# New instruction lengths and distances in the list scheduler of a decoder trunk's odd layer

## The chip, the cores and the metric

The kernel runs on one core of a Trainium2 chip. The metric is the device time of one execution in microseconds; the median of three runs of the kernel before is 2234.52 us (2234.44 to 2235.84). The core has five engines that work through their own queues in order: TensorE (PE, with its weight loads PEld), VectorE (DVE), ScalarE (ACT), GpSimd (POOL) and SyncE (SP), which here issues the DMAs. An engine waits for another by semaphores.

## What is computed

A trunk of two residual layers on x of 1024 tokens by 1024 features, float32, then a last RMS norm. The even layer (dilated attention and a gated linear recurrence) is not touched. The odd layer, cut to what matters:

```python
qkv, z, b_logit, a_logit = split(hn @ w_in)            # 4096, 2048, 16, 16 columns
qkv = silu(causal_depthwise_conv(qkv, conv_w))         # 4 taps
q, k, v = split(qkv)                                   # 8 heads of q and k, 16 of v, 128 wide
q, k = l2_normalize(q) * 128 ** -0.5, l2_normalize(k)
beta, g = sigmoid(b_logit), -exp(a_log) * softplus(a_logit + dt_bias)
# chunked delta rule: S_t = exp(g_t)(I - b_t k_t k_t^T) S_{t-1} + b_t k_t v_t^T ; o_t = S_t^T q_t
sol = triangular_solve(lower + eye, rhs)               # per chunk
v_new = u_n - w_n @ state; o = qd_n @ state + a_n @ v_new
state = state * gl_n + kt_n^T @ v_new
o = rms_norm(o, norm_w) * silu(z)
h = h + o @ w_out
out = rms_norm(h, final_norm_w)
```

## The kernel before, in words

The odd layer works on eight pairs of heads hh = 0 to 7 (one k and q head with its two v heads) and on eight chunks of 128 tokens each. Weights come as 128 x 512 pieces through `cut` (line 323): SP loads `raww`, ACT rounds it into `w_hi`, DVE subtracts into `w_lo`. Every projection is three fp32r matmul passes of 512 columns (hi x hi, hi x lo, lo x hi), 24 matmuls for half the tokens, in one of two PSUM banks with the tag `pj`. For each head there are these generators, which write their instructions in small steps:

- `proj(j)` (line 1182): first `way_out(j - 2)`, then the projections of k of head j + 1 (`pk`), of the two v heads (`pv`) and of q (`pq`). Each goes through `conv` (line 1103): ACT copies both halves into the single buffer `ub` (uk, uv, uq in the trace), scales one tap, DVE adds three taps with three dependent steps, ACT takes the tanh, and a last DVE step gates (kT, vT, q). `turn_q`, `turn_k` and `turn_v` transpose on PE (tq, tk, tv) and scale (`bv`, `sc`, `kn`); `turn_k` has a chain of small DVE steps (rn, rt).
- `invert(hh)` (line 1255): the triangular inverse. Sixteen DVE steps make L from kk, ACT gathers Lg, DVE transposes it into Lp, and a loop of 31 (line 1292) takes two dependent DVE steps each: tm from Lp and Tp, then Tp less tm. tm has one buffer. Two DVE transposes (Tn, Un) follow, and small matmuls (qp, up, q, u in the trace) put the blocks together in U, kept in the tile L.
- `recur(hh)` (line 1360): for each chunk, PE makes ks and qs from the state S, DVE makes r from ks, ACT makes oq from qs, PE makes vp from r and U, DVE makes vt and ACT makes vn from vp, PE makes kv from vt, and DVE makes the next S from kv. Beside this PE makes op from vn and qk for the next chunk, DVE adds bv and makes A, ACT squares bv into oj.
- `way_out(hh)` (line 1228): norm of bv on DVE (ors, ort) and POOL, the projection of z (`oz`), its gate g (one buffer), transposes ot, and on ACT, POOL and SP the product oy, which goes to `ymix` in DRAM. `out_last` (line 1466) reads `ymix` back (rawy, yplo), multiplies with the output weights (op from w_hi and w_lo) and adds into the residual hr.

`mix` (line 366) and `blend` (line 376) interleave these in program order: `recur(hh)` with `invert(hh + 1)` and `proj(hh + 1)`; ahead of the loop stand the gates, the projections of head 0 and `invert(0)`.

That program order is only the start. In the odd layer every call to an engine goes to `Plan.add`, and `plan.run()` (line 1492) makes a list schedule of all five queues. `edges` finds what each operation must wait for; for each reuse of a buffer it adds a gate, which opens when all users of the old tile are done. `times` (line 107) gives each operation two numbers: how long its engine is held, and when its result is there. `run` takes, again and again, the engine that can start first, and on it the ready operation that stands first in program order. `release` (line 227) says from when a follower may start: the end of what it waits for and a distance `SEM` (line 90) by the follower's engine. Line 270 then issues all operations in the order of their modelled starts. On the chip each queue runs in that order, whatever the true times are. Line 284 records the same calls in the even layer, which has no plan.

Of the kernel before, what the change touches and what calls it, by code (L numbers as in the profile page):

```python
# [16 lines left out]
PSUM = bass.MemoryType.PSUM  # L17
# [64 lines left out]
class Plan:  # L82
# [4 lines left out]

    SEM = {"PE": 500, "DVE": 300, "ACT": 300, "POOL": 300, "SP": 300}  # L90

    def __init__(self):
        self.ops = None
# [12 lines left out]

    def times(self, op, last):

        key, name, a = op["key"], op["name"], op["a"]
        n = self.elems(op["out"][0])  # L110
        if key == "SP":
            return 420, 3200
        if key == "PE":
            if name == "transpose":
                return 109, 280
            r32 = a[1].dtype == F32R
            rows, cols = a[2].ap[0][1], self.elems(a[1])
            small = rows < 128 or cols < 128
            if small:
                held = 2.0 * (8 if cols == 32 else 18)  # L120
            else:
                held = n / 2.4 * (1 if r32 else 4) + (14 if r32 else 8)
            if small != last.get("small", False):
                held += 120
            last["small"] = small
            return held, held + 190
        if key == "DVE":
            if name == "transpose":
                t = 1950 if n >= 1024 else 1070 if op["out"][0].ap[-1][0] != 1 or a[1].ap[-1][0] != 1 else 620
            elif name == "memset":  # L130
                t = 60 + 0.82 * n
            elif n < 20:
                t = 85
            elif n >= 512:
                t = 100 + 1.15 * n
            else:
                t = 70 + 1.08 * n
            return t, t + 80
        if key == "ACT":
            t = 210 + 0.75 * n if n > 128 else 300  # L140
            if "accum_out" in op["kw"]:
                t = 440
            return t, t + 95
        if name == "memset":
            return 560, 600
        t = 780 if n <= 256 or a[0].ap[0][1] == 32 else 1330
        return t, t + 40

    def edges(self):
        ops = self.ops  # L150
# [52 lines left out]
    def run(self):  # L203
        ops = self.ops
        pred, gates = self.dag = self.edges()
        n = len(ops)
        succ = [[] for _ in range(n + len(gates))]
        deg = [0] * (n + len(gates))
        for i, ps in enumerate(pred):
            for j in ps:  # L210
                succ[j].append(i)
                deg[i] += 1
        for g, (old, new, _) in enumerate(gates):
            inner = set(new)
            for j in old:
                succ[j].append(n + g)
                deg[n + g] += 1
            for i in new:
                if not pred[i] & inner:
                    succ[n + g].append(i)  # L220
                    deg[i] += 1
        keys = ("PE", "DVE", "ACT", "POOL", "SP")
        ready = {k: [] for k in keys}
        free = {k: 0.0 for k in keys}
        at = [0.0] * (n + len(gates))

        def release(j, done, key):
            for i in succ[j]:
                k = ops[i]["key"] if i < n else None
                if k is None or k == key and k not in ("PE", "SP"):  # L230
                    t = done
                else:
                    t = 0.0 if k == key == "PE" else done + self.SEM[k]
                at[i] = max(at[i], t)
                deg[i] -= 1
                if not deg[i]:
                    if i < n:
                        ready[k].append(i)
                    else:
                        release(i, at[i], None)  # L240

        for i in range(n):
            if not deg[i]:
                ready[ops[i]["key"]].append(i)
        last, starts, done_n, ends = {}, [0.0] * n, 0, [0.0] * n
        while done_n < n:
            best = None
            for k in keys:
                if ready[k]:
                    s = max(free[k], min(at[i] for i in ready[k]))  # L250
                    if best is None or s < best[0]:
                        best = s, k
            if best is None:
                raise RuntimeError("the order of the tiles' places does not work out")
            s, k = best
            i = min(i for i in ready[k] if at[i] <= s)
            ready[k].remove(i)
            held, got = self.times(ops[i], last)
            starts[i] = s
            free[k] = s + held  # L260
            ends[i] = s + got
            release(i, s + got, k)
            done_n += 1
        self.starts, self.ends = starts, ends
# [1298 lines left out]
```

## Time and profile before

| what | value |
|---|---|
| median of 3 runs | 2234.52 us |
| the profiled execution | 2235.39 us |
| its span, first to last instruction | 2233.6 us |
| mean granted clock of TensorE | 0.979 |
| PE, PEld busy | 2162.9 us (97%), 1780.9 us (80%) |
| DVE, ACT, POOL busy | 1393.5 us (62%), 947.2 us (42%), 239.2 us (11%) |

The profile is of one execution. Its times count from the span's start; the page cuts the span into 40 slices of 56 us and gives the busy tenths of each engine in them. The granted clock is the share of full speed at which PE was allowed to run. The first projections of the odd layer run at about 1240 us. A row of the timeline has start, length, engine, line, operation, output and inputs, shapes and count; in brackets stands how long the engine was idle before it and what ended that. The operations of the odd layer have line 270, so they are told apart by their tiles.

### The profile page before, as it was taken

To read this page: it belongs to the slowest core of one execution; us is meant where nothing else is said; L and a number is where in the kernel's file an instruction comes from. 1 tells how busy PE (TensorE), PEld (TensorE's weight loads), DVE (VectorE), ACT (ScalarE), POOL (GpSimd) and SP (SyncE) were. 2 spreads that over 40 slices of the span, in tenths; PEclk is the share of its full clock that TensorE was granted. 3 is DMA by queue.
4 is the path that set the end of the run, shared out by engine and by line. 5 is a ranking of instruction groups with operands and counts; after the bars stand their busy time and mean duration, and the time that the engine had idled before them with its cause. 6 is when DMAs were issued, how large, how long until landed. Compare 5 with 4: busy or idle time off the path is not lost. (4 is left out here: it accounts for less than half of the span.)

```text
span 2233.6 us, 52459 instructions
## 1 busy us (share of the span) xinstructions
PE 2162.9 (97%) x21781; PEld 1780.9 (80%) x21781; DVE 1393.5 (62%) x3236; ACT 947.2 (42%) x2551; POOL 239.2 (11%) x252
## 2 busy tenths in 40 slices
PE   7999999999999999989998998899999999999998
PEld 6888888888787878767786776788888888887886
DVE  6353545453444444446666798697897988865677
ACT  6233333333223222222124855657566565653223
POOL 0011111110000000000000001312212121130100
PEclk9999999999999999989998998799999999999999
DMA  4111111114333434362233212212213121224223
GB/s 149 39 49 45 48 44 49 49 39 122 84 102 93 114 104 115 92 171 88 92 100 108 87 46 55 70 48 79 79 57 83 49 83 53 83 74 150 89 95 123
DMA packets 100078, 184.14 MB, mean 82 GB/s; under 512 B 12672, under 2 KB 30208, under 8 KB 99840
## 3 DMA queue, kind: packets, MB, share of 16 engines
q1 hardware_dynamic: 99840, 180.79, 26.5%
q8 instruction: 171, 2.80, 0.5%
q14 instruction: 67, 0.55, 0.1%
HBM read 151.25 MB, written 29.49 MB: 81 GB/s over the span
## 5 line engine op out<-in xcount | busy, mean ns | idle before, releaser
L284 DVE TENSOR_TENSOR w_lo<-raww,w_hi 128x512 fp32r<-128x512 f32 x160 | 117.9, 740 | 150.0 <-ACT w_hi L284 149.5
L284 ACT CAST w_hi<-raww 128x512 fp32r<-128x512 f32 x160 | 99.4, 621 | 203.7 <-DMA raww<-in_ewo_dram 54.2
L270 PE MATMUL op<-w_hi,yplo 128*128 128x512 f32 x448 | 140.4, 392 | 0.7 <-DVE hr L270 0.6
L284 ACT ACTIVATE P<-P,nm 128x256 f32<-128x256 f32 (+7 forms) x128 | 71.4, 559 | 133.4 <-DVE nm L284 133.3
L270 ACT CAST w_hi<-raww 128x512 fp32r<-128x512 f32 x132 | 81.8, 621 | 89.8 <-DMA raww<-in_owo_dram 42.8
L270 DVE TENSOR_TENSOR hr<-hr,op 128x512 f32<-128x512 f32 x128 | 87.4, 685 | 48.7 <-PE op L270 46.2
L284 PE MATMUL op<-w_hi,yphi 128*128 128x512 f32 x320 | 105.9, 405 | 7.9 <-DVE hres L284 4.8
L270 DVE TENSOR_TENSOR w_lo<-raww,w_hi 128x512 fp32r<-128x512 f32 x132 | 96.3, 732 | 20.5 <-ACT w_hi L270 17.5
L270 PE MATMUL pv<-hn_hi,w_hi 128*128 128x512 f32 x256 | 107.4, 419 | 0.0
L270 PE MATMUL oz<-hn_hi,w_hi 128*128 128x512 f32 x256 | 107.3, 419 | 0.0
L270 PE MATMUL pv<-hn_hi,w_lo 128*128 128x512 f32 x256 | 103.6, 405 | 0.0
L270 PE MATMUL pv<-hn_lo,w_hi 128*128 128x512 f32 x256 | 102.4, 400 | 0.0
L270 PE MATMUL oz<-hn_hi,w_lo 128*128 128x512 f32 x256 | 102.2, 399 | 0.0
L270 PE MATMUL oz<-hn_lo,w_hi 128*128 128x512 f32 x256 | 101.9, 398 | 0.0
L284 DVE STREAM_TRANSPOSE PB<-P 128x256 f32<-128x256 f32 (+3 forms) x64 | 54.6, 853 | 72.9 <-ACT P L284 72.9
L270 PEld LDWEIGHTS op<-w_hi,yplo 128*128 128x128 f32 x448 | 84.1, 188 | 18.9 <-DVE hr L270 1.5
L270 POOL TENSOR_TENSOR gca<-gca,MA 128x256 f32<-128x256 f32 x64 | 54.6, 854 | 366.0 <-DMA gca<-gcd 196.3
L270 PE MATMUL op<-w_lo,yplo 128*128 128x512 f32 x224 | 86.9, 389 | 0.0
L284 DVE TENSOR_TENSOR hres<-hres,op 128x512 f32<-128x512 f32 x96 | 64.7, 682 | 31.7 <-PE op L284 30.9
L284 DVE CUSTOM_DVE_ANT_0 P<-S,G 128x256 f32<-128x256 f32 (+7 forms) x128 | 58.1, 491 | 36.8 <-PE S L284 36.5
L284 PEld LDWEIGHTS op<-w_hi,yphi 128*128 128x128 f32 x320 | 62.0, 194 | 23.8 <-DVE hres L284 5.6
L284 PE MATMUL avp<-w_hi,hn_hi 128*128 128x256 f32 x256 | 74.6, 291 | 0.0
(345 smaller groups left out, 6352.6 us busy)
## 6 DMA issues: line engine op xcount, KB each, us to landing
raww<-in_ew_dram SPq DMA_DIRECT2D x128, 256.0 KB, 3.0
raww<-in_ow_dram SPq DMA_DIRECT2D x100, 256.0 KB, 3.0
V<-vd SPq DMA_DIRECT2D x64, 256.0 KB, 5.3
rawy<-ymix SPq DMA_DIRECT2D x64, 256.0 KB, 2.7
raww<-in_ewo_dram SPq DMA_DIRECT2D x32, 256.0 KB, 3.0
gcl<-gcd SPq DMA_DIRECT2D x64, 128.0 KB, 3.2
gca<-gcd SPq DMA_DIRECT2D x64, 128.0 KB, 3.0
ymix<-oy SPq DMA_DIRECT2D x32, 256.0 KB, 2.8
```

Of the source, the lines that this page charges most:

```text
L270: ops[i]["f"](*ops[i]["a"], **ops[i]["kw"])
L284: return f(*a, **kw)
```

## The change

It touches `Plan` alone. No operation is added or removed; the numbers from which the order is made are others:

- `SEM`: 300 ns instead of 500 into PE, 150 instead of 300 into the other engines.
- `times`: other lengths, by more kinds. Among them: a DVE step of 512 elements 603 ns (656 for one with three inputs) instead of 689; a small one of 128 elements by scalar_tensor_tensor 260 ns instead of 208; an ACT copy of 512 elements 476 ns from PSUM and 522 from SBUF instead of 594; a result with a sum beside it 230 ns after the engine is free instead of 95; small matmuls 28 and 62 ns instead of 16 and 36; a switch between small and large matmuls 100 ns instead of 120; a DMA 430 and 3100 ns instead of 420 and 3200.
- `release`: a follower on the same engine (SP left out) may start as soon as the engine is free. Before, that held for PE; on DVE, ACT and POOL it waited for the modelled end, some 40 to 95 ns after the engine was free. A gate still adds its distance, on the same engine too.

```diff
-    SEM = {"PE": 500, "DVE": 300, "ACT": 300, "POOL": 300, "SP": 300}
+    SEM = {"PE": 300, "DVE": 150, "ACT": 150, "POOL": 150, "SP": 150}
...
         if key == "SP":
-            return 420, 3200
+            return 430, 3100
...
             if small:
-                held = 2.0 * (8 if cols == 32 else 18)
+                held = 28 if cols == 32 else 62
             else:
-                held = n / 2.4 * (1 if r32 else 4) + (14 if r32 else 8)
+                held = n / 2.4 * (1 if r32 else 4) + (17 if r32 else 8)
             if small != last.get("small", False):
-                held += 120
+                held += 100
...
-            elif n < 20:
-                t = 85
+            elif n < 24:
+                t = 82
+            elif out.ap[0][1] == 32:
+                t = 715
             elif n >= 512:
-                t = 100 + 1.15 * n
+                t = (65 if name == "scalar_tensor_tensor" and len(op["ins"]) == 3 else 12) + 1.155 * n
+            elif name == "scalar_tensor_tensor":
+                t = 260
             else:
-                t = 70 + 1.08 * n
-            return t, t + 80
+                t = 72 + 1.03 * n
+            return t, t + 83
         if key == "ACT":
-            t = 210 + 0.75 * n if n > 128 else 300
-            if "accum_out" in op["kw"]:
-                t = 440
-            return t, t + 95
+            if n < 24:
+                t = 200
+            elif op["ins"][0].space == PSUM:
+                t = 249 if n <= 128 else 268 if n <= 256 else 0.93 * n
+            else:
+                t = 293 if n <= 128 else 307 if n <= 256 else 1.02 * n
+            if n >= 512 and (len(op["ins"]) > 1 or out.ap[0][1] == 32):
+                t += 100
+            return t, t + (230 if "accum_out" in op["kw"] else 110)
...
-                if k is None or k == key and k not in ("PE", "SP"):
+                if k is None:
                     t = done
                 else:
-                    t = 0.0 if k == key == "PE" else done + self.SEM[k]
+
+                    t = 0.0 if k == key != "SP" else done + self.SEM[k]
```

More of the change, by code (lines that the diff above doesn't have):

```diff
@@ L107, in times @@
     def times(self, op, last):
-        key, name, a = op["key"], op["name"], op["a"]
-        n = self.elems(op["out"][0])
+        key, name, a, out = op["key"], op["name"], op["a"], op["out"][0]
+        n = self.elems(out)
         if key == "SP":
-            return 420, 3200
+            return 430, 3100
         if key == "PE":
             if name == "transpose":
-                return 109, 280
+                return 109, 290
             r32 = a[1].dtype == F32R
@@ L128, in times @@
             if name == "transpose":
-                t = 1950 if n >= 1024 else 1070 if op["out"][0].ap[-1][0] != 1 or a[1].ap[-1][0] != 1 else 620
+                t = 1980 if n >= 1024 else 1060 if op["out"][0].ap[-1][0] != 1 or a[1].ap[-1][0] != 1 else 620
             elif name == "memset":
-                t = 60 + 0.82 * n
-            elif n < 20:
-                t = 85
+                t = 60 + 0.86 * n
+            elif n < 24:
+                t = 82
+            elif out.ap[0][1] == 32:
+                t = 715
             elif n >= 512:
-                t = 100 + 1.15 * n
-            else:
-                t = 70 + 1.08 * n
-            return t, t + 80
+                t = (65 if name == "scalar_tensor_tensor" and len(op["ins"]) == 3 else 12) + 1.155 * n
+            elif name == "scalar_tensor_tensor":
+                t = 260
+            else:
+                t = 72 + 1.03 * n
+            return t, t + 83
         if key == "ACT":
-            t = 210 + 0.75 * n if n > 128 else 300
-            if "accum_out" in op["kw"]:
-                t = 440
-            return t, t + 95
+            if n < 24:
[7 more added lines that the diff above has]
+            return t, t + (230 if "accum_out" in op["kw"] else 110)
         if name == "memset":
-            return 560, 600
-        t = 780 if n <= 256 or a[0].ap[0][1] == 32 else 1330
-        return t, t + 40
+            return 565, 565
+        t = 750 if n <= 256 or out.ap[0][1] == 32 else 1010 if len(op["ins"][1].ap) > 2 else 1250
+        return t, t + 50
     def edges(self):
```

## The prediction

> **What bounds the kernel now.** I read the page first, for the engines' shares and the slices:
>
> ```profile
> span 2233.6 us, 52459 instructions
> PE   7999999999999999989998998899999999999998
> PEclk9999999999999999989998998799999999999999
> ```
>
> The profiled execution took 2235.39 us, 1.8 us more than its span; the median of the runs shown is 2234.52 us, 0.87 us less. TensorE (PE) is busy in nearly every slice of 56 us. The change touches the odd layer alone, whose first projection runs at about 1246 us, so I cut the rest into stages with the windows view (columns: stretch, its length, busy us of PE, PEld, DVE, ACT and POOL, granted clock, DMA share, GB/s):
>
> ```profile
> 1246.00:1360.00 114.00, 109.38 (x723) 89.77 (x722) 100.60 (x262) 70.49 (x193) 10.35 (x13) 0.99 0.24 66
> 1360.00:1420.00 60.00, 47.73 (x378) 37.91 (x377) 41.82 (x137) 25.92 (x83) 14.58 (x19) 0.66 0.14 39
> 1420.00:2030.00 610.00, 607.97 (x4298) 507.59 (x4297) 494.82 (x1351) 371.84 (x1127) 132.27 (x144) 1.00 0.24 71
> 2030.00:2050.00 20.00, 15.51 (x66) 12.54 (x65) 8.84 (x19) 6.65 (x17) 0.87 (x1) 0.86 0.73 271
> 2050.00:2220.00 170.00, 169.32 (x761) 139.67 (x761) 121.72 (x202) 44.22 (x85) 10.12 (x8) 1.00 0.27 90
> 2220.00:2233.60 13.60, 5.41 (x24) 4.13 (x22) 10.27 (x19) 6.02 (x14) 0.00 (x0) 0.82 0.59 231
> ```
>
> Busy time times granted clock is PE work in full-clock microseconds; what is missing to the length of the stretch is lost. 1246 to 1360: 114 - 109.38 x 0.99 = 5.7 us. 1360 to 1420: 60 - 47.73 x 0.66 = 28.5 us. 1420 to 2030, more than half of the layer: 610 - 607.97 = 2.0 us. 2030 to 2050: 20 - 15.51 x 0.86 = 6.7 us. 2050 to 2220: 0.7 us. The last 13.6 us are the final normalisation, behind the last matmul. So the layer is PE-bound but for one pocket. An order can win at most 5.7 + 28.5 + 2.0 + 6.7 + 0.7 = 43.6 us, and two thirds of it lie in 60 us. In the seven heads behind the pocket there is next to nothing to win and much to lose.
>
> What is the pocket? The timeline of PE, in its middle, shows one chunk of the recurrence of head 0 and nothing else:
>
> ```profile
> 1385.42 1.19 PE L270 MATMUL ks<-S,kT 128*128 128x256 f32 x2
> 1386.40 1.06 PE L270 MATMUL qs<-S,q 128*128 128x256 f32 x2
> 1388.24 1.23 PE L270 MATMUL vp<-r,L 128*128 128x128 f32 x4 [0.78 <-ACT oq L270]
> 1389.98 0.80 PE L270 MATMUL op<-vn,A 128*128 128x128 f32 x2 [0.52 <-ACT vn L270]
> 1390.57 1.09 PE L270 MATMUL kv<-vt,kn 128*128 128x256 f32 x2
> 1392.45 0.76 PE L270 MATMUL ks<-S,kT 128*128 128x256 f32 x1
> ```
>
> From ks to ks 1392.45 - 1385.42 = 7.0 us. No projection matmul fills the gaps: head 1's projections are used up, and the gate projection of head 0 (oz, in `way_out`) can go no further than its buffers, because its result is multiplied with the normed output of that very recurrence. PE waits for a chain: recurrence 0, then its norm, beside inversion 1 on DVE. What that chain ends, ends the pocket. All PE work ahead of that point is a fixed sum, so each microsecond by which the chain ends earlier is a microsecond of the kernel, until the 28.5 us are used up.
>
> The clock makes it dearer. In a full stretch these multiplications take half as long, by the critical view:
>
> ```profile
> 1343.99 0.43 PE kv L270 x2
> ...
> 1346.47 0.43 PE ks L270 x2
> 1346.90 0.43 PE qs L270 x2
> ...
> 1386.61 0.87 PE qs L270 x2
> ...
> 1390.78 0.88 PE kv L270 x2
> ```
>
> qs and kv need 0.43 us ahead of the pocket and 0.87 and 0.88 us in it. The longest idle that the timeline gives for that chunk is 0.78 us. The Trainium skill ("TensorE: Matmul & The Clock Gate", section "HAM oscillation — how this bites in real kernels") gives as its rule that idle gaps of PE must stay under about 3.4 us for the clock to stay up. By it such short gaps would leave the clock alone, the pocket would cost only its idle time, 60 - 47.73 = 12.3 us, and the term for the clock in the sum below would be 0 instead of -1 us; the granted clock of 0.66 does not agree, and I go by the 28.5 us.
>
> **The change part by part.** The same instructions run; only their order on the five queues changes. The scheduler takes, on the engine that can start first, the ready operation that stands first in the program. It has three new things.
>
> *One: an operation whose input comes from its own engine no longer waits for the modelled end, only until the engine is free.* Until now a dependent DVE step was ready 80 ns after the engine, so any other ready step, however late in the program, slipped in between. The timeline of DVE in the inversion of head 0 shows it:
>
> ```profile
> 1288.91 0.23 DVE L270 TENSOR_TENSOR tm<-Lp,Tp 128x78 f32<-128x78 f32 x1
> 1289.06 0.68 DVE L270 TENSOR_TENSOR bv<-tv,sc 128x512 f32<-128x512 f32 x1
> 1289.66 0.23 DVE L270 TENSOR_TENSOR Tp<-Tp,tm 128x78 f32<-128x78 f32 x1
> 1289.90 0.75 DVE L270 SCALAR_TENSOR_TENSOR q<-uq,cws,q 128x512 f32<-128x512 f32 x1
> 1290.57 0.26 DVE L270 TENSOR_TENSOR tm<-Lp,Tp 128x100 f32<-128x100 f32 x1
> ```
>
> Of tm, other, Tp, other, tm the two others take most of the time. Over the whole inversion, from the transpose Lp to Un, the windows view gives all of DVE and then the steps on tm alone, for head 0 and for a later head:
>
> ```profile
> 1279.40:1325.40 46.00, 42.31 (x123) 1.00 0.11 36
> 1622.00:1663.70 41.70, 39.22 (x129) 1.00 0.18 54
> 1279.40:1325.40 46.00, 16.16 (x62) 1.00 0.11 36
> 1622.00:1663.70 41.70, 17.07 (x62) 1.00 0.18 54
> ```
>
> The 62 steps need 16.2 us and are spread over 46.0. With the three transposes 65 of 123 instructions are the inversion's, so 58 others stand between. The new rule closes one of the two openings: Tp follows its tm at once. The other stays, because the next tm reuses the one tm buffer and its place is released with a distance (83 + 150 = 233 ns, before 80 + 300 = 380 ns). So about 31 openings instead of 62. Taking the mean other at (42.31 - 16.16) / 61, with the transposes in it, 0.43 us, 58 - 31 = 27 of them go behind: 27 x 0.43 = 11.6 us. Against that stands what back-to-back dependence costs on the chip:
>
> ```profile
> 1387.24 0.34 DVE L270 SCALAR_TENSOR_TENSOR r<-ks,sc,bv 128x128 f32<-128x128 f32 x1
> 1387.50 0.27 DVE L270 TENSOR_TENSOR tm<-Lp,Tp 128x121 f32<-128x121 f32 x1
> 1387.81 0.28 DVE L270 TENSOR_TENSOR Tp<-Tp,tm 128x121 f32<-128x121 f32 x1
> ```
>
> r takes 0.34 us but tm starts 0.26 us after it; Tp, which needs tm, starts 0.31 us after a tm of 0.27. So a dependent neighbour costs about 0.12 us more than a stranger: 31 x 0.12 = 3.7 us if all 31 pairs become neighbours. (The Trainium skill, "VectorE: DVE Perf Modes", section "The DRAIN you can't avoid", has the next operation start only when the pipe is empty, whatever the chaining; by that the 3.7 us would be 0 and the bound below -11.6 us. The overlap of r and tm does not agree.) Inversion 0 thus shortens by up to 11.6 - 3.7 = 7.9 us. But recurrence 0 also needs q, bv and vT of head 0, which are among the 58: those put behind come due anyway. Bounds for its start: 0 and -7.9; I take -4, the middle, as the others are of both sorts (vT, q and bv of head 0, kT of head 2).
>
> In the pocket the same rule works on inversion 1 beside recurrence 0. Four chunks bring 4 x 7 = 28 DVE steps (r twice, vt, S twice, A, bv), about as many as the 31 openings, so both should still end together: 0, with bounds of -3 and +3 (half a step of the recurrence, 0.34 us, won or lost at each of some 18 places).
>
> *Two: distances between engines, 500 to 300 ns into PE and 300 to 150 ns into the others, and lengths by kind.* What the chip needs is far less: S below ends at 1392.31 and the next ks starts at 1392.45, 0.14 us, where the old plan held 80 + 500 and the new one holds 83 + 300.
>
> ```profile
> 1391.70 0.61 DVE L270 SCALAR_TENSOR_TENSOR S<-S,g_egl,kv 128x128 f32<-128x128 f32 x2
> L270 DVE TENSOR_TENSOR w_lo<-raww,w_hi 128x512 fp32r<-128x512 f32 x122 | 89.5, 736 | 8.0 <-ACT w_hi L270 5.0 <-PE ot L270 2.0 <-PE tv L270 0.6
> L270 PE MATMUL pv<-hn_hi,w_hi 128*128 128x512 f32 x256 | 107.4, 419 | 0.0
> L270 PE MATMUL pv<-hn_hi,w_lo 128*128 128x512 f32 x256 | 103.6, 405 | 0.0
> ```
>
> Six crossings into PE or out of it per chunk (ks to r to vp to vt to kv to S to ks) shorten in the plan, so the plan puts recurrence steps sooner and fewer fillers before them. In the pocket, where nothing else is in line on PE, the chip starts them when they are ready in either order: 0. A single DVE step of 512 was planned at 100 + 1.15 x 512 = 689 ns, now at 603; the row gives 736 ns of duration, less the overlap. Where PE is saturated such truer lengths move nothing that ends last: 0. The stream is broken as often as before, since the number of recurrence steps is the same; the first matmul of a triple shows what a break costs, 419 against 405 ns, 256 x 14 ns = 3.6 us for pv. A tenth more or fewer breaks in all projections is about 1 us: bounds -1 and +1.
>
> *Three: the chip's clock follows.* If the pocket ends 4 us sooner, half a chunk less runs at the low clock. A chunk at full clock is shorter by 0.44 us in qs and kv each; taken for ks and vp too, that is 1.8 of 7.0 us; 4 / 7.0 x 1.8 = 1.0 us. I take -1, bounds 0 and -2.
>
> *Other places.* The stretch ahead of the pocket loses 5.7 us, where DVE (100.60 of 114 us) is the nearest competitor; with its dependent steps no longer shared out to strangers I take -1, bounds -3 and +2. At 2030 to 2050 PE stands behind transfers (271 GB/s there against 71 before); the plan keeps one fixed time for a transfer (3200, now 3100 ns) and can see no queue, so the stall stays: 0, bounds -5 and +3. The head of SP's queue holds 430 instead of 420 ns: nothing. Saturated middle: 0, but here is the risk, next.
>
> Sum: -4 + 0 + 0 - 1 - 1 = -6. On the profiled run 2235.39 - 6 = 2229.4; on the median 2234.52 - 6 = 2228.5 us. About 0.2% (4.5 us) is what a measurement of this kernel can tell from no change.
>
> **The rivals.**
>
> *The pocket does not move.* DVE is the second resource in it: 41.82 of 60 us busy, and 100.60 of 114 before it. If what ends the pocket is the sum of DVE work of head 0, head 1 and inversion 1, its inner order is indifferent, and steps put behind the inversion come due before the recurrence all the same. Then only the -1 of the early stretch is left: 2233.5 us. For it: the idle share of DVE before the pocket is only 12%. Against: kT of head 2 and its norm, which stood within inversion 0, are not needed before recurrence 0.
>
> *Slower: the convolutions starve behind the inversion.* In each of the later heads the inversion's steps stand early in the program, and its openings now go to the lowest number, mostly recurrence steps. In the old order conv steps (kT, vT) took many. PE can run ahead of conv only by its two `pj` banks and the one `ub` buffer that ACT fills, two halves each: a half is 24 matmuls at 0.23 us, 5.5 us, so 11 us in the banks and up to 11 in `ub`. An inversion of 41.70 us with 39.22 busy shortens to perhaps 33 us without conv; in it PE also has some 11 us of recurrence work. It decides from the point at which conv is shut out for longer than 11 + 5.5 + 11 = 27.5 us, with one half of `ub` filled on average. At 33 us PE would lack up to 5.5 us; some 2 us in each of six heads is +12, and with the early gain eaten as well 2234.52 + 12 = 2246.5 us. For it: the plan now also reckons a dependent neighbour of 121 elements at 72 + 1.03 x 121 = 197 ns where the chip shows 310 (the old one reckoned 201 + 80), so the real DVE runs behind the plan by 3.5 us per inversion. Against: DVE is busy 494.82 of 610 us in the middle, so it has 19% to catch up, and PE, whose breaks the plan does not count, runs behind the plan too.
>
> *Slower: recurrence 0 is held behind inversion 1.* If the pairs tm and Tp go ahead of r and S in the pocket, each of 4 chunks grows by a pair, 0.6 us, in a pocket whose chunks take 7.0 / 5.2 = 1.35 of their full-clock time: 4 x 0.6 x 1.35 = +3.2 us and, with the gain of the start lost, about 2238.
>
> **How the numbers follow.** The forecast, an earlier end of the pocket by 2 to 14 us, has 0.47, and nearly all of that is faster by over 0.2%. The unmoved pocket has 0.29, the starved conv 0.15, the held recurrence 0.09. Cases of gain: 0.46 faster; 0.30 same; 0.24 slower. The low end takes the bounds of the start (-7.9), of the pocket (-3), the clock (-2) and half of the early stretch and the transfers (-5), -18: 2216. The high end takes the starved conv, nearly: 2245.
>
> **What would show it.** In the changed profile: inversion 0 (Lp to Un) under 42 us instead of 46.0; the first ks earlier than 1346.47; the pocket's lost time near 22 us instead of 28.5; the stretch of the later heads still within 0.5% of full. It would be wrong if the inversion is shorter but the recurrence starts no sooner (first rival), or if PE waits for ACT's copy of pk, pv or pq, or for DVE's conv steps, appear in the middle (second).

## The result and the profile after

The changed kernel takes 2299.59 us (median of 5 runs, 2297.81 to 2300.77) against 2234.52 us: 65 us more, a ratio of 1.0292 with a 95% interval of [1.0277, 1.0307]. A gain of 6 us had been forecast. The page of the profile after, its head:

```profile
span 2298.0 us, 52517 instructions
PE 2181.9 (95%) x21781; PEld 1774.7 (77%) x21781; DVE 1436.3 (63%) x3236; ACT 952.6 (41%) x2551; POOL 236.9 (10%) x252
```

The matmuls are as many as before (21781), and so are the DVE instructions (3236), but DVE is busy for 42.8 us more and PE for 19.0 us. The stages by the windows view, columns as in the prediction; the stretches behind 2030 us are moved with the work:

```profile
1246.00:1360.00 114.00, 103.54 (x692) 82.24 (x691) 101.38 (x261) 73.11 (x202) 9.76 (x14) 0.99 0.24 66
1360.00:1420.00 60.00, 53.89 (x413) 41.48 (x412) 45.47 (x139) 24.25 (x77) 14.00 (x17) 0.77 0.13 40
1420.00:2030.00 610.00, 564.08 (x3987) 453.46 (x3987) 501.55 (x1276) 346.13 (x1032) 117.15 (x130) 0.99 0.21 62
2030.00:2090.00 60.00, 59.28 (x302) 50.05 (x301) 30.22 (x73) 28.61 (x90) 13.23 (x13) 1.00 0.26 85
2090.00:2110.00 20.00, 16.01 (x73) 12.85 (x73) 8.63 (x18) 6.45 (x18) 1.62 (x2) 0.95 0.69 261
```

The pocket from 1360 to 1420 loses 60 - 53.89 x 0.77 = 18.5 us instead of 28.5. The middle, which lost 2.0 us in 610, now loses 610 - 564.08 x 0.99 = 51.6 us. That is where most of the change lies.

Where exactly? Inversions 2 and 7 begin at 1435.9 and 1968.8 us after the change, at 1441.6 and 1915.7 before it. Between them lie five heads, with nearly the same work (the matmul records differ by 25 of 3432). The rows of before and after:

```profile
1441.60:1915.70 474.10, 472.07 (x3407) 393.62 (x3406) 401.15 (x1109) 295.89 (x890) 103.76 (x112) 1.00 0.23 67
```
```profile
1435.90:1968.80 532.90, 493.03 (x3432) 396.20 (x3431) 435.84 (x1109) 300.04 (x900) 101.72 (x112) 0.99 0.21 61
```

Up to inversion 2 the changed kernel is 5.7 us ahead. The five heads cost 532.9 - 474.1 = 58.8 us more, 11.8 per head, and what lies behind them 11.3 us more; -5.7 + 58.8 + 11.3 = 64.4 us is the difference of the spans. In the five heads the same 1109 DVE instructions keep DVE busy for 435.84 instead of 401.15 us. PE is idle for 39.9 us instead of 2.0.

What PE waits for, from the waits view of after (who, for whom, us in total, times, longest):

```profile
PE kv L280 <- DVE vt L280: 15.3, 16, 1.5
PE ks L280 <- DVE S L280: 13.1, 15, 1.8
PE kk L280 <- DVE L L280: 10.1, 11, 1.5
PE vp L280 <- ACT oq L280: 8.1, 8, 3.8
```

Before, the same waits were these:

```profile
PE vp L270 <- ACT oq L270: 7.8, 5, 4.5
PE kk L270 <- DVE L L270: 2.8, 1, 2.8
PE kv L270 <- DVE vt L270: 1.2, 2, 0.9
PE ks L270 <- DVE tm L270: 1.2, 2, 0.8
PE ks L270 <- DVE S L270: 1.0, 1, 1.0
```

Both lists are for the whole odd layer. In the five heads alone kv waits for 12.5 us, ks for 10.2, kk for 7.2 and vp for 4.0; before, kv waited there for 0.9, kk for 0.6, ks for 0.4 and vp not at all. These are steps of the recurrence and of the next inversion's matrix, all behind DVE or ACT; no projection is among them. One of these waits, in the timelines of DVE, POOL and PE of after (head 3, at the end of its inversion; rows left out are marked by dots):

```profile
1668.69 0.16 DVE L280 TENSOR_SCALAR cq<-qss 128x8 f32<-128x8 f32 x1
1668.77 0.74 DVE L280 SCALAR_TENSOR_TENSOR kT<-uk,cws,kT 128x512 f32<-128x512 f32 x1
1669.43 0.77 DVE L280 TENSOR_TENSOR tm<-Lp,Tp 128x70 f32<-128x70 f32 x1
...
1671.43 0.69 DVE L280 TENSOR_TENSOR w_lo<-raww,w_hi 128x512 fp32r<-128x512 f32 x1
1672.03 0.20 DVE L280 TENSOR_TENSOR tm<-Lp,Tp 128x45 f32<-128x45 f32 x1
1672.27 0.20 DVE L280 TENSOR_TENSOR Tp<-Tp,tm 128x45 f32<-128x45 f32 x1
1672.39 0.74 DVE L280 SCALAR_TENSOR_TENSOR kT<-uk,cws,kT 128x512 f32<-128x512 f32 x1
1673.05 0.18 DVE L280 TENSOR_TENSOR tm<-Lp,Tp 128x30 f32<-128x30 f32 x1
1673.27 0.19 DVE L280 TENSOR_TENSOR Tp<-Tp,tm 128x30 f32<-128x30 f32 x1
1673.37 0.42 DVE L280 TENSOR_TENSOR vt<-vp,g_etl 128x256 f32<-128x256 f32 x1
```
```profile
1669.29 0.83 POOL L280 TENSOR_TENSOR gca<-gca,MA 128x256 f32<-128x256 f32 x1 [8.14 <-DMA gca<-gcd]
```
```profile
1668.45 0.71 PE L280 MATMUL vp<-r,L 128*128 128x128 f32 x4
...
1672.41 0.40 PE L280 MATMUL pv<-hn_lo,w_hi 128*128 128x512 f32 x1
1673.85 0.70 PE L280 MATMUL kv<-vt,kn 128*128 128x256 f32 x2 [1.03 <-DVE vt L280]
```

vp ends at 1669.2, but vt, the DVE step on it, stands behind the inversion's steps, three steps of conv and w_lo, and starts at 1673.37. DVE does not idle; it is late. One of the inversion's steps, the tm at 1669.43, takes 0.77 us where others of its size take 0.23; it runs beside the operation of POOL. The plan put kv where it thought vt done, and PE, which keeps the plan's order, stands before kv for 1.03 us, with projections (pv) behind it in its queue.

The prediction's point on the inversion came out: from Lp to Un inversion 0 lasts 37.2 us instead of 46.0, a later one 33.2 instead of 41.7.

```profile
1278.30:1315.50 37.20, 36.00 (x98) 1.00 0.13 43
1643.10:1676.30 33.20, 31.82 (x97) 1.00 0.18 53
```

Of 98 instructions 65 are the inversion's; 33 others stand between, where the prediction counted 31 openings.

### The profile page after: what moved, and what is told of

Read it like the earlier page. It is cut to its first block, busy times and chain, and to the rows that moved or that the text cites. A ratio compares the mean times of both kernels' runs of the same rounds, so it can differ in the third digit from the quotient of the medians.

```text
span 2298.0 us, 52517 instructions
## 1 busy us (share of the span) xinstructions
PE 2181.9 (95%) x21781; PEld 1774.7 (77%) x21781; DVE 1436.3 (63%) x3236; ACT 952.6 (41%) x2551; POOL 236.9 (10%) x252
## 5 line engine op out<-in xcount | busy, mean ns | idle before, releaser
L294 DVE TENSOR_TENSOR w_lo<-raww,w_hi 128x512 fp32r<-128x512 f32 x160 | 118.0, 740 | 149.6 <-ACT w_hi L294 149.4
L280 DVE TENSOR_TENSOR w_lo<-raww,w_hi 128x512 fp32r<-128x512 f32 x132 | 91.5, 702 | 39.8 <-ACT w_hi L280 37.6
L280 DVE TENSOR_TENSOR hr<-hr,op 128x512 f32<-128x512 f32 x128 | 86.7, 685 | 46.1 <-PE op L280 45.3
L280 PEld LDWEIGHTS op<-w_hi,yplo 128*128 128x128 f32 x448 | 84.1, 188 | 18.5 <-DVE hr L280 1.1
L280 DVE SCALAR_TENSOR_TENSOR vT<-uv,cws,vT 128x512 f32<-128x512 f32 x96 | 75.5, 787 | 6.6 <-ACT vT L280 4.8
```

Source lines behind the costliest of these rows:

```text
L280: ops[i]["f"](*ops[i]["a"], **ops[i]["kw"])
L294: return f(*a, **kw)
```

## The experiments

The change has three parts: the release rule (R), the lengths (L) and the distances (D). Each time below stands beside the kernel before on the same chip.

**One part undone, or one alone.** e1 puts the old release rule back into the changed kernel:

```diff
-                if k is None:
+                if k is None or k == key and k not in ("PE", "SP"):
...
-                    t = 0.0 if k == key != "SP" else done + self.SEM[k]
+                    t = 0.0 if k == key == "PE" else done + self.SEM[k]
```

> The change with the old release rule put back: new lengths and new distances, but a follower on DVE, ACT and POOL waits for its predecessor's modelled end again. Theory A (the release rule alone: dependent DVE neighbours cost 0.12 us each that the plan does not count, so DVE falls behind the plan and PE stands in line for it): back to 2225 to 2245 us. Theory B (the shorter distances leave PE no margin): stays at 2280 to 2300 us. Theory C (the new lengths, above all ACT's shorter ones): stays at 2280 to 2300 us.

2251.00 against 2232.27 us, 1.0076 [1.0061, 1.0091]: +18.7 us. Taking the rule away removes the greater part of the loss, but lengths and distances together cost something too; the time lies between the theories' ranges.

e2 is the kernel before with the new rule alone (e1's diff the other way round).

> The kernel before with the new release rule alone. Theory A: 2280 to 2300 us, the whole loss. Theory B or C: 2225 to 2245 us.

2257.35 us, 1.0109 [1.0094, 1.0124]: +25.1 us. Theory A had 2280 to 2300; the rule alone is less than half of the loss.

e3 and e4 are the kernel before with the new `SEM` line alone and with the new `times` alone.

> The kernel before with the new distances alone (300 ns into PE, 150 into the others). Theory B: 2270 to 2300 us. Theory A or C: 2225 to 2245 us.

2241.92 us, 1.0041 [1.0026, 1.0056]: +9.7 us.

> The kernel before with the new lengths alone. Theory C: 2270 to 2300 us. Theory A or B: 2225 to 2245 us.

2238.94 us, 1.0027 [1.0017, 1.0037]: +6.7 us. So B and C fall as sole causes. The parts add up to 25.1 + 9.7 + 6.7 = 41.5 us, and L and D together (18.7) are near their sum (16.4), so 65 - 41.5 = some 23 us come from the rule meeting the others. e7, the changed kernel with the old distances (R and L), asks which.

```diff
-    SEM = {"PE": 300, "DVE": 150, "ACT": 150, "POOL": 150, "SP": 150}
+    SEM = {"PE": 500, "DVE": 300, "ACT": 300, "POOL": 300, "SP": 300}
```

> The changed kernel with the old distances: new release rule and new lengths. If the parts only add up: 2232.3 + 25.1 + 6.7 = 2264 us. If the distances are the margin that hides DVE's falling behind the plan (so that short ones and the new rule make each other worse), the whole excess of the three parts together, 67 less 25, 10 and 7, goes with them: 2255 to 2268 us. If the excess lies between rule and lengths instead: 2280 to 2290 us.

2283.42 against 2233.86 us, 1.0227 [1.021, 1.0244]: +49.6 us, where 25.1 + 6.7 = 31.8 would be the sum. The excess lies mostly between rule and lengths.

**Which engine's rule.** e6 leaves the new rule to ACT and POOL and makes DVE followers wait again.

```diff
-                if k is None:
+                if k is None or k == key == "DVE":
```

> The changed kernel with the old release rule for DVE only; on ACT and POOL a follower may still start at once. If DVE's part of the rule makes the loss: 2245 to 2256 us, as with the whole old rule (2251.0), and about 39 dependent neighbours per head on DVE. If ACT's and POOL's part makes it: 2285 to 2300 us.

2254.53 us, 1.0095 [1.008, 1.011]: +20.7 us, as e1 within the intervals. So it is DVE's part of the rule that costs.

**Does the plan's ignorance cost the time, or the order?** The prediction had measured that a dependent DVE step starts some 0.12 us later than a stranger. The old rule had reckoned 80 ns for it, the new one nothing. e5 leaves the changed kernel as it is and lets the plan start a DVE operation 115 ns later when its direct predecessor is the one just before it:

```diff
             held, got = self.times(ops[i], last)
+            if k == "DVE" and before.get(k) in pred[i]:
+                s += 115
+            before[k] = i
```

> The changed kernel, but its plan starts a DVE operation 115 ns later when the one just before it on DVE is its direct predecessor, which is what the traces show. Release rule, lengths and distances stay new. Theory A1 (the loss comes from the plan not knowing this price: it puts PE's steps too early, and PE stands in line for DVE): back to 2235 to 2260 us, PE idle per head from 8.0 to under 3 us. Theory A2 (the order itself, first in program first on DVE with some 50 more neighbours per head, costs the time): stays at 2280 to 2300 us.

2267.49 us, 1.0154 [1.0138, 1.0169]: +33.6 instead of +65 us. Half of the loss is gone by one number in the plan. The time lies between the two theories' ranges, and PE's idle time per head in the five heads is 4.0 us, where theory A1 had under 3. e8 does the same to the rule alone (e2 with e5's lines).

> The kernel before with the new release rule, and a plan that starts a DVE operation 115 ns later behind its direct predecessor; old lengths and distances. Theory A1: 2225 to 2243 us, against 2257.4 of the rule alone. Theory A2: 2252 to 2262 us.

2241.64 us, 1.0037 [1.0022, 1.0052]: +7.8 instead of +25.1 us. A1's range is met.

**Through whose lengths.** e11 and e12 give the changed kernel the old block of lengths for DVE or for ACT.

> The changed kernel with the old DVE lengths; ACT, PE, POOL and DMA lengths, rule and distances stay new. Rule and lengths together cost 18 us more than one by one (2283.4 with old distances, against 25.1 + 6.7 alone). If that comes from DVE's own lengths, whose old figure for 512 elements (689 ns) held some of the neighbour's price that 603 and 656 ns no longer hold: 2268 to 2285 us. If it comes from ACT's shorter ones: 2292 to 2302 us.

2285.61 against 2233.31 us, 1.0234 [1.022, 1.0248]: +52.3 us, 13 less than the change and 0.6 us above the range for DVE.

> The changed kernel with the old ACT lengths; all else new. If rule and lengths hurt each other through ACT (512 elements planned at 476 to 522 ns instead of 594): 2268 to 2285 us. If through DVE: 2292 to 2302 us.

2292.97 us, 1.0263 [1.0249, 1.0277]: +59.7 us, 5 less, in the range for DVE. So it is mostly DVE's lengths. A likely reason, not shown by itself, is that 689 ns for 512 elements held some of the neighbour's price that 603 and 656 ns, true for strangers, no longer hold.

**What holds the other half.** Three kinds of slack, each on top of e5: e13 has the old distances, e14 charges 125 ns for a dependent neighbour on ACT too, e15 charges 230 instead of 115 ns on DVE.

> The changed kernel with 115 ns charged for a dependent DVE neighbour, and with the old distances. If the rest of the loss, 34 us at 2267.5 us, is the margin that short distances take away: 2240 to 2256 us. If the distances do nothing once the price is known: 2262 to 2270 us.

2252.94 against 2234.17 us, 1.0087 [1.0073, 1.0101]: +18.8 us.

> The changed kernel with 115 ns charged for a dependent neighbour on DVE and 125 ns on ACT, the step between the two peaks of ACT's gaps in the traces (100 ns of overlap, 30 ns of idle). If the rest of the loss is this price on ACT: 2240 to 2258 us. If not: 2262 to 2272 us.

2254.26 us, 1.0095 [1.0077, 1.0113]: +20.1 us.

> The changed kernel with 230 instead of 115 ns charged for a dependent DVE neighbour, twice what the traces show. If DVE falls behind the plan by more than the price, and any slack in the plan helps: 2240 to 2258 us. If the plan's knowledge of DVE is now true and the order itself, first in program first, costs the rest: 2262 to 2275 us.

2251.44 us, 1.0072 [1.0056, 1.0088]: +17.3 us. Each of them took away 13 to 16 us and met the first range of its expectation; so none can be the one cause. e17 has all three at once:

> The changed kernel with 230 ns charged for a dependent neighbour on DVE, 125 ns on ACT, and the old distances; release rule and lengths stay new. If the whole loss comes from a plan that is faster than the chip: 2228 to 2242 us. If the order, first in program first with more neighbours on DVE, costs a part by itself: 2245 to 2255 us, no better than each slack alone (2251.4 to 2254.3).

2239.87 against 2233.35 us, 1.0027 [1.0015, 1.0039]: +6.5 us, which is what the new lengths cost alone (+6.7). With the new rule and the new lengths in place, a plan that is slow enough loses almost nothing. The five heads of e1, e5 and e17, from inversion 2 to 7, by the windows view:

```profile
1435.80:1926.80 491.00, 476.31 (x3393) 391.36 (x3392) 410.36 (x1102) 294.61 (x890) 100.88 (x111) 1.00 0.22 65
```
```profile
1434.80:1939.60 504.80, 484.77 (x3428) 395.31 (x3427) 426.17 (x1105) 301.08 (x898) 103.16 (x112) 1.00 0.22 64
```
```profile
1437.90:1920.60 482.70, 475.70 (x3404) 396.07 (x3403) 417.22 (x1109) 295.33 (x889) 101.73 (x113) 0.99 0.23 66
```

e17 has 417.22 us of DVE, 16 us more than the kernel before, and by the gaps in the trace still 64 dependent neighbours on DVE per head, against 29 before and 81 after the change. Yet its heads cost only 1.7 us more each. So it is neither the busier DVE nor the order with more neighbours by itself that loses the time.

But slack is not good by itself. e18 is e17 with the old lengths (689 ns instead of 603 or 656 for a DVE step of 512 elements):

> The kernel before with the new release rule, and 230 ns on DVE and 125 ns on ACT charged for a dependent neighbour; old lengths and distances. If the whole loss of the rule is the plan's error: 2224 to 2234 us, against 2241.6 with 115 ns on DVE alone, with the gain at the start left over. If the order costs a part: 2238 to 2246 us.

2280.39 us, 1.0207 [1.019, 1.0224]: +47.0 us, outside both ranges. Its five heads, and PE's waits over the odd layer:

```profile
1437.10:1957.30 520.20, 502.94 (x3437) 418.94 (x3436) 419.23 (x1110) 302.07 (x903) 101.60 (x113) 0.95 0.21 62
```
```profile
PE q L274 <- ACT L L274: 6.1, 5, 2.1
PE vp L274 <- ACT oq L274: 6.0, 4, 4.1
PE u L274 <- DVE Q L274: 3.6, 4, 1.0
```

DVE is hardly busier than in e17 (419.23), but PE now waits in the small matmuls of the inversion (q, u), and the granted clock falls to 0.95 in the five heads. Of the 46.1 us that these heads cost more than before, some 15 are idle time (17.3 against 2.0 us) and some 25 are the clock (502.94 x 0.05). So the larger part of e18's loss is not waiting in line behind DVE, but the lower clock. Why this order brings it about was not settled.

**Distances the other way.** e10 is the kernel before with 700 ns into PE and 450 into DVE, ACT and POOL.

> The kernel before with longer distances: 700 ns into PE, 450 into DVE, ACT and POOL. If a distance is a margin that keeps PE from standing in line, more of it costs the middle nothing (PE is full there) and the pocket a little: 2228 to 2240 us, PE idle per head not above 0.5 us. If 500 and 300 are merely a setting that fits, and any other order loses: 2240 to 2255 us.

2237.68 us, 1.0018 [1.0009, 1.0027]: +4.4 us, in the first range: more margin costs little. Of the three settings tried, 500 and 300 ns are the best.

**The forecast's own gain, alone.** e9 is the kernel before with the new rule up to the recurrence of head 0 in program order, and the old rule behind; e16 adds e5's charge there.

```diff
-                if k is None or k == key and k not in ("PE", "SP"):
+                if k is None or k == key and k not in ("PE", "SP") and i >= self.mark:
...
             drain(fill)
+            if not hh:
+                plan.mark = len(plan.ops)
```

> The kernel before with the new release rule only for operations up to and with the recurrence of head 0 in program order; old rule behind, old lengths and distances throughout. If the forecast's own gain is real (the pocket ends sooner) and only the later heads lose: 2221 to 2229 us, inversion 2 about 10 us sooner than in the kernel before (1441.6 us), later heads at 94 to 96 us each. If the gain at the start is paid back behind it: 2232 to 2238 us.

2229.59 us against 2233.31, 0.9983 [0.9974, 0.9992]: -3.7 us, 0.6 us above the range of the first case. This is the fastest order found, and only e16 beside it also beats the kernel before. From the first projection to inversion 2, and the five heads behind:

```profile
1246.00:1430.20 184.20, 164.59 (x1175) 134.82 (x1174) 155.87 (x416) 110.94 (x319) 28.21 (x35) 0.92 0.23 67
1430.20:1907.60 477.40, 475.83 (x3430) 397.23 (x3429) 404.89 (x1109) 296.88 (x894) 104.20 (x113) 1.00 0.24 67
```

Inversion 2 begins at 1430.2, 11.4 us sooner than before, and the heads cost 95.5 us each, as expected; they give back 3.3 us. The profiled execution ends 7.7 us sooner, the medians differ by less.

> The kernel before with the new release rule up to the recurrence of head 0, and 115 ns charged there for a dependent DVE neighbour; the old rule behind. If the plan's error costs time at the start too: 2221 to 2227 us, better than 2229.6 without the charge. If PE's order at the start hangs on nothing the charge moves: 2228 to 2232 us.

2231.70 against 2234.17 us, 0.9988 [0.9979, 0.9997]: -2.5 us, the same as e9 within the intervals. At the start the charge brings nothing more.

## Why the prediction was wrong

*What bounds the kernel* was right: a pocket of 28.5 us to win from, and a full middle with "next to nothing to win and much to lose".

*The start*, the sum of -6, came out by luck: inversion 2 begins 5.7 us sooner, but not in the forecast way. Inversion 0 was forecast under 42 us and takes 37.2, and the first ks, at 1346.31 in PE's timeline before, comes at 1339.15: 7.2 us sooner, where -4 was taken and -7.9 was the bound. This lead does not last. The seventh ks, the last of head 0, comes at 1393.25 instead of 1392.45. From the first to the seventh it takes 54.1 us instead of 46.1, where "both should still end together" gave 0, with bounds of -3 and +3. In the last chunk the end of inversion 1 stands in the way:

```profile
1388.30 1.22 PE L280 MATMUL kv<-vt,kn 128*128 128x256 f32 x2 [0.53 <-DVE vt L280]
1389.06 1.07 DVE L280 STREAM_TRANSPOSE Tn<-Tp 128x512 f32<-128x512 f32 x1
1390.16 0.71 DVE L280 STREAM_TRANSPOSE Un<-Tn 128x512 f32<-128x512 f32 x1
1390.91 1.58 DVE L280 COPY L<-Un 32x512 f32<-32x512 f32 x2
1392.50 0.60 DVE L280 SCALAR_TENSOR_TENSOR S<-S,g_egl,kv 128x128 f32<-128x128 f32 x2
```

kv ends at 1389.5, but S, which needs it, starts at 1392.50. The pocket loses 18.5 us where 22 was forecast for another reason: PE has other work there. By the windows view with oz alone, PE runs 71 matmuls of the gate projection between 1360 and 1420 instead of 32, and none of them ahead of 1360, where it ran 43 before. So the stretch ahead loses 114 - 103.54 x 0.99 = 11.5 instead of 5.7 us, where -1 had been taken. Two errors nearly cancel. In e9 the chain itself does end sooner, as forecast: its seventh ks comes at 1385.80, 6.7 us ahead, and -3.7 us of the -6 stay in the time. (The low end of the forecast's range adds 5 us for "half of the early stretch and the transfers", where half of -3 and -5 is -4; nothing hangs on it.)

*The step that failed* is "Where PE is saturated such truer lengths move nothing that ends last: 0", and with it "Saturated middle: 0". It was argued from the chip's view: the middle is full, distances are longer than the chip needs, so shorter ones do no harm. The new rule had no term of its own in the later heads either; there it stood only in a rival, and alone it costs 25.1 us (e2). But the order is fixed by the plan, and PE stays full only as long as each step it comes to is ready. The long distances, the long 689 ns and the wait of a follower were, taken together, room: they let the plan bring PE to a step later than the chip needed. The change took all three away at once. Then DVE came late (vt at 1673.37), PE stood before kv, and what PE loses there no later slack returns. The runs show it by putting room back in different places: 115 ns per neighbour takes 65 to 34 us, any of three further kinds to 17 to 20, all of them to 6.5. That more room always helps is not shown; e18 speaks against it.

*The rival of the starved conv* had the right sign, and among its reasons the right cause: that the plan reckons a dependent neighbour at 197 ns where the chip shows 310. It priced the wrong consequence. ACT's waits for conv did grow, from 23.2 to 44.1 us for uv:

```profile
ACT uv L280 <- DVE vT L280: 44.1, 30, 5.8
ACT uk L280 <- DVE kT L280: 34.3, 14, 4.9
```

but PE's waits are for the recurrence, and a head loses 11.8 us where 2 were taken. That DVE "has 19% to catch up" was the argument that made the rival small. It is an average: in the rows above DVE does not idle while PE waits for vt. Of the two other rivals, the unmoved pocket is out, since the pocket loses 10 us less. The recurrence held behind inversion 1 did come about, by 8.0 us from the first to the seventh ks where +3.2 had been priced, but the gate projection filled PE meanwhile, and the pocket still lost less than before.

*The price of a neighbour* (0.12 us) held. The five heads show it at large: counted in the trace, 81 instead of 29 DVE steps per head start 25 to 40 ns behind the end of the step before them, where most others start some 80 ns ahead of it. That makes 52 x 0.12 = 6.2 us per head. DVE is busier by (435.84 - 401.15) / 5 = 6.9 us per head, but this is not the same thing: of the price only the lost overlap, 0.08 us, counts as busy, 52 x 0.08 = 4.2 us. Most of the rest are steps that themselves take longer beside an operation of POOL, like the tm above: in the five heads 53 steps last over 60 ns longer than the median of their kind away from POOL, before it was 31, and every one of them overlaps an operation of POOL. All steps beside POOL together last 26.4 us longer than that median, before it was 14.5: 2.4 us more per head. No run charged the plan for that, so what it adds to the loss is not known. The prediction quoted from the Trainium skill's "VectorE: DVE Perf Modes", section "The DRAIN you can't avoid", that the next operation starts only when the pipe is empty, whatever the chaining; by that a neighbour would cost 0, and these rows do not agree. The same section adds that a next operation that is not held starts earlier, and with the 80 ns of the others the trace agrees.

What stays open: why slack on top of the old lengths (e18) brings the low clock and loses 47 us, and so how near a plan must be to the chip on either side.

## What to carry to other kernels

Numbers in a scheduler that fixes the order of in-order queues are not only estimates: what they exceed the chip by can be the room that keeps the bottleneck engine from standing in line, so a truer number can make a worse order. But room is not better without limit (e10 loses 4 us and e18 47). Before a rule is loosened and margins are cut, look for costs that the model leaves out (here 0.12 us for each dependent neighbour on DVE) and put them in first. Where one stretch has something to win and another only to lose, change the rule for that stretch alone.

## What the runs showed of the hardware

PE's busy time took up a part of the waits. In the five heads PE is busy for 472.07 us before and 493.03 us after at nearly the same clock (1.00 and 0.99), 21 us more, beside 38 us more of idle time that the profile shows. A little of the 21 us is work that falls on the other side of the stretches' ends (24 more matmuls of pk, 10 fewer of oz). Another view is the time from the start of the matmul ahead to a step's own start. For kv, ks, kk and vp it grew by 43.5 us in all; 33.1 us of that is shown as idle, and some 10 us lie inside the records of the matmuls ahead. The first matmul of a triple shows how little of the loss lies in the projections, 419 ns before against 427 after:

```profile
L280 PE MATMUL pv<-hn_hi,w_hi 128*128 128x512 f32 x256 | 109.2, 427 | 0.0
```

PE's loss had better be read from the length of equal work than from its idle time alone.

DVE steps beside an operation of POOL can take far longer. In the five heads of all 20 traces, 824 of 3759 DVE steps that overlap one last over 60 ns longer than the median of their kind without it; of the 18071 others it is one.

ACT shows two states as DVE does. In the odd layer the largest group of its operations (716 of 1567 before, 690 after) begins 85 to 105 ns ahead of the end of the one before it. A second group, 41 before and 151 after, begins 25 to 40 ns behind that end, and most of it needs the result of the operation just before it; the step between the two is where e14's 125 ns come from.
